# A new order for the first block's list of steps: attention units one by one, one gate later, recurrent preparation earlier

## The chip, the cores and the metric

The kernel runs on one core of one Trainium2 chip. The metric is device microseconds from start to end of the program. A core has five engines that run side by side, each through its own fixed sequence of instructions: TensorE (PE, matrix products), VectorE (DVE), ScalarE (ACT), GpSimd (POOL) and SyncE (SP, which issues the loads of the weights). They wait for each other through semaphores.

## What is computed

Two transformer-like blocks on one sequence of 256 tokens and width 1024, all in fp32. Only the first half of the first block is touched by the change:

```python
xn = rms_norm(x, norm1_w)
q, k_c, v_c, k_s, v_s, k_w, v_w, g_nsa, xr, gr, g_a, g_b = split(xn @ w_in)
attn = nsa_attention(q, ...)      # compressed + two causal branches, 8 heads
rnn = rg_lru_branch(xr, gr, ...)  # conv, gates, linear scan, times gelu(gr)
merged = sigmoid(g_a) * (attn @ w_up_attn) + sigmoid(g_b) * (rnn @ w_up_rnn)
x = x + merged @ w_out
```

The recurrent branch is `a = exp(c * r)`, `b = sqrt(1 - a^2) * (i * xc)`, `h[t] = a[t] h[t-1] + b[t]`, where `r` and `i` are sigmoids of small block products of the convolved input `xc` and `c` is a function of `lru_lambda` alone. The compressed attention needs a small two-layer network over the keys and values first. Behind this half come an MLP and the whole second block, which the change leaves alone.

## The kernel before

All products are made with operands split in two fp32r parts, a high and a low one, and three products each. The activations u are split once. The weights come in raw pieces of up to 128x1024, and each piece is split when it is wanted: ACT copies it to `whi` (line 260), DVE subtracts to get `wlo` (line 261). Five pieces of either can stand ready. PE then takes a product of 128 output rows pair by pair (`mmx`, line 324): a step such as `ga0` is 48 matmuls with 256 columns, and DVE (and for a gate ACT, a tanh) empties the PSUM bank.

The order of the first block is written by hand in `ORDER_1` (line 158), a string of words. Each word becomes a step (or several), and the steps are called one after the other; their weight blocks are packed into pieces in the same order. The list does not fix the order of the instructions: the program is built under `tile.TileContext(nc, schedule_with_timeline_sim=True)`, which orders the instructions of each engine at build time, by what it expects to be ready, with the order of the calls as priority. Where the kernel wants an order for certain it ties one instruction behind another of the same engine (`behind`, no semaphore).

The words:

- `xr0` to `xr3`, `gr0` to `gr3`, `ga0` to `ga3`, `gb0` to `gb3`: products with w_in, two column blocks each. `ga` and `gb` are the gates of the attention and of the recurrent branch, `xr` and `gr` the input and the gate of the recurrent one.
- `cmp_x`, `cw0` to `cw7`, `cmp_hT`, `cmp_fin`, `cmp_w2`, `cmp_attn`: the compression network and its attention (scores `cmps`, one exponential, probabilities).
- `atN`: the next N units of a queue of sixteen attention units. With j from 0 to 3 (pairs of heads) a unit is s0j or s1j (`nsa_scores`: scores of the first or second half of the tokens in the PSUM banks "s", of which there are two; a minimum per row on DVE, line 824; exponentials on ACT through line 287, six for s0j and two for s1j; scaling on DVE, line 835) or t0j or t1j (`nsa_T`: transposes on PE, line 843, then the split `pt..h` on ACT, line 354, and `pt..l` on DVE, line 355). The queue is s00 s10 t00 s01 t10 s11 t01 s02 t11 s12 t02 s03 t12 s13 t03 t13. Unit t0j reads s0j alone, unit t1j reads s0j and s1j.
- `pv`: the next of four products of probabilities and values (line 909); the second and the fourth also add the compressed part and split the result into `q`.
- `prep` (`rnn_prep`, line 921): c from lru_lambda, 27 small steps on POOL with 8 columns each, two sigmoids on ACT and three small steps on DVE; its first step is tied behind the norm's power on POOL.
- `lru0` to `lru3`: block products into the banks "s", two sigmoids each (ra, ig), a tanh with c (rt). Then `exp` (ra again, squares, rt), `sqrt` (rt), `bt` (xc, line 1003), `gelu` (rg), and `scan0` to `scan3`: two scans (line 1015), a product with rg (line 1016), and the split into `rnn` (lines 354 and 355).
- `mb0` to `mb3` (m1b, reads all of rnn) and `ma0` to `ma3` (m1a, reads q): the upward projections.

ACT has one table of functions loaded at a time. `G.table` (line 287) therefore puts the calls into groups by table, in the order of the list, and ties each call behind every call of the group before. Tanh is in several tables and joins the group that is open; copies and squares are free.

Of the kernel before, what the change touches and what calls it, by code (L numbers as in the profile page):

```python
# [10 lines left out]
AF = mybir.ActivationFunctionType  # L11
# [3 lines left out]
P = 128  # L15
# [139 lines left out]

ORDER_1 = """norm cst xr0 kv_fin q_fin k0 ties q1 cmp_x ga0 cw0 vg0 cw1 xr1 cw2 at1 ga1 cw3 prep cw4 xr2 cw5 at1 ga2 cw6 cw7 xr3 cmp_hT cmp_fin
cmp_w2 gr0 cmp_attn at2 lru0 lru1 ga3 at1 lru2 lru3 at1 gr1 at1 gr2 pv0 at1 gr3 exp sqrt bt at1 gelu gb0 pv0 at1 scan0 at1
scan1 gb1 gb2 scan2 at2 scan3 gb3 at1 mb0 at1 mb1 pv0 at1 mb2 pv0 mb3 ma0 ma1 ma2 ma3"""  # L160
ORDER_2 = """qs0 qs1 qe0 qe1 nb ka0 ka1 va at1 qb0 at1 qb1 at2 kb at3 ga0 at3 ga1 at3 ga2 at3 ga3 at3 gb0 at2 gb1 at2 gb2 at1
ma0 gb3 ma1 mb0 ma2 mb1 ma3 mb2 mb3"""

# [31 lines left out]
class Prog:  # L195
# [154 lines left out]
    def split2(self, hi, lo, src, scale=1.0):  # L350

        nc = self.nc
        if isinstance(scale, float) and scale == 1.0:
            nc.scalar.activation(out=hi, in_=src, func=AF.Copy)
            nc.vector.tensor_tensor(out=lo, in0=src, in1=hi.bitcast(F32), op=ALU.subtract)
        else:
            nc.scalar.activation(out=hi, in_=src, func=AF.Copy, scale=scale)
            nc.vector.scalar_tensor_tensor(out=lo, in0=src, scalar=scale, in1=hi.bitcast(F32), op0=ALU.mult, op1=ALU.subtract)


    def fm(self, tag, name, nk, npair, x, evac, rows=None, cols=None, lead=2, hold=2, after=None):
# [38 lines left out]
def build(nc, tc, d, out, es, dbg=None):  # L400
# [22 lines left out]
    G = Prog(nc, tc, pools, d, dbg)  # L423
    one = pools["one"]
    V = {}
    S = {}
# [410 lines left out]
    def probs_T(name, tiles, dst):  # L837

        for s in range(2):
            pt = G.ps("t", f"pt{name}{s}")  # L840
            ts = tiles(s)
            for e, t in enumerate(ts):
                nc.tensor.transpose(pt[:, e * P:(e + 1) * P], t, S["ident"])
            h, l = dst(s)
            G.split2(h, l, pt[:, :len(ts) * P])

    def rr_pair(name, n):
        return [[pools["rr"].tile([P, 768], F32R, tag="rr", name=f"{name}{s}{a}")[:, :n] for a in "hl"] for s in range(2)]
# [38 lines left out]
    def nsa_T(br, j):  # L887
        a = S[f"at0{j}"]
        if br == 0:
            tiles = lambda s: [a[:, s, 0:P], a[:, s, T:T + P], a[:, s, T + P:2 * T]]  # L890
        else:
            w = S[f"at1{j}"]
            tiles = lambda s: [a[:, s, P:T], w[:, s, 0:P], w[:, s, P:T]]
        if j % 2 == 0:
            S["pt", br] = rr_pair(f"pt{br}{j}", 768)
        c = 384 * (j % 2)
        probs_T(f"n{br}{j}", tiles, lambda s: [x[:, c:c + 384] for x in S["pt", br][s]])
# [107 lines left out]
    def rnn_gelu():  # L1005
        for h in range(2):
            sl = slice(4 * h, 4 * h + 4)
            G.table("gelu", out=S["rg"][:, sl, :], in_=S["rg"][:, sl, :], func=AF.Gelu_apprx_tanh)

    def rnn_scan(p):  # L1010
        sl = slice(2 * p, 2 * p + 2)
# [57 lines left out]
    def first():  # L1069

        rows = (("kcvc", lambda n: [((512, 640)[n], P)]), ("q", lambda n: [(n * 64, 64), (256 + n * 64, 64)]))

        def fn():
            S["kcvc"], S["q0"] = G.ps("g", "kcvc0"), G.ps("s", "q0")
            for k in range(8):
                ws = [(S[key][:, nn * T:(nn + 1) * T], *G.wt((tag, k, nn)), nn) for key, tag in (("kcvc", "kcvc"), ("q0", "q"))
                      for nn in range(2)]
                x = xu(k)
                for o, wh, wl, nn in ws:
                    for a in range(2):  # L1080
                        nc.tensor.matmul(o, wh, x[:, a, :], start=k + nn + a == 0, stop=False, skip_group_check=True)
                for o, wh, wl, nn in ws:
                    nc.tensor.matmul(o, wl, x[:, 0, :], start=False, stop=k == 7, skip_group_check=True)

        G.step(fn, [((tag, k, n), W1, [(k * P, P)], cols(n)) for k in range(8) for tag, cols in rows for n in range(2)])
# [49 lines left out]
    first()  # L1135
    for w in ORDER_1.split():
        if w in STEPS_1:
# [311 lines left out]
    def b2_T(kind, j):  # L1449
        nm_ = f"{kind}{j}"  # L1450
        t = S["at" + nm_]
        pts = S["pt" + nm_] = rr_pair("pt" + nm_, 512)
        probs_T(nm_, lambda s: [t[:, s, i * T + kb * P:i * T + (kb + 1) * P] for kb in range(2) for i in range(2)], lambda s: pts[s])
# [189 lines left out]
```

## Time and profile before

| | us |
|---|---|
| median of 3 runs | 967.04 (966.53 to 969.43) |
| the profiled execution | 966.44 |
| its span, first to last instruction | 964.7 |
| PE busy | 946.2 (98%) |
| DVE busy | 730.2 (76%) |
| ACT busy | 588.0 (61%) |
| mean granted PE clock | 0.994 |

A busy share is a mean over the whole span: the stage that the change touches lies in the first 230 us and is loaded otherwise than the rest. The granted clock is 1.00 at 2.4 GHz and 0.50 at 1.2 GHz. Consecutive matmuls overlap in the records, so that a matmul of 0.28 us may start 0.12 us behind the one before.

### The profile page before, as it was taken

The page shows a single profiled execution, that of the slowest core. Times are in us where ns is not written, and L with a number is a line of the kernel's source. Part 1 is how long each engine was busy: PE and PEld are TensorE (multiplying, and loading weights), DVE is VectorE, ACT ScalarE, POOL GpSimd, SP SyncE. Part 2 cuts the span into 40 slices and gives each one's busy share as a digit, 9 for nine tenths or more (in the row PEclk, how much of TensorE's full clock was granted, in tenths as well). Part 3 has the DMA queues.
Part 4 walks back from the last instruction along what each step waited for, and adds up shares of the span by engine and source line. Part 5 has one row for each costly group of instructions (what it writes and reads, how often), then busy time and mean ns, then how long its engine had stood idle before and what let it go on. Part 6 is the DMA issues. An engine that isn't in the chain of part 4 may idle for free.

```text
span 964.7 us, 15748 instructions
## 1 busy us (share of the span) xinstructions
PE 946.2 (98%) x6176; PEld 862.7 (89%) x6176; DVE 730.2 (76%) x1219; ACT 588.0 (61%) x966; POOL 46.6 (5%) x72
## 2 busy tenths in 40 slices
PE   9999997999999999999999999999999999999996
PEld 8999997998888888888888888999999888888885
DVE  7999779878787755569888666779877878878553
ACT  6896599446666644446555444588974566555541
POOL 1117000000000000021000200000000000000000
PEclk9999998999999999999999999999999999999999
DMA  9667342445545555557455755363334565555541
GB/s 337 227 222 259 131 176 88 158 137 188 199 176 184 203 181 175 190 185 227 175 197 196 212 197 190 125 232 124 126 132 135 175 226 186 193 199 173 180 158 43
DMA packets 28138, 174.01 MB, mean 180 GB/s; under 512 B 3488, under 2 KB 4768, under 8 KB 9120
## 3 DMA queue, kind: packets, MB, share of 16 engines
q1 hardware_dynamic: 26208, 169.07, 50.2%
q0 software_dynamic: 1136, 2.63, 1.3%
q10 hardware_dynamic: 720, 1.31, 0.4%
q8 instruction: 48, 0.79, 0.3%
q14 instruction: 26, 0.21, 0.1%
HBM read 171.43 MB, written 1.05 MB: 179 GB/s over the span
## 4 chain that ended last, share of the span: by engine, by line
PE 92%; ACT 4%; DVE 2%; issue 1%; DMA 0%; SPq 0%; POOLq 0%; POOL 0%; ACTq 0%
PE f L331 17%; PE w L331 12%; PE f L332 9%; PE w L332 6%; PE ld L318 6%; PE ga L324 5%; PE fd L331 4%; PE wo L331 3%; PE gb L324 3%; PE gr L324 2%; PE m1b L324 2%; PE fd L332 2%; PE xr L324 2%; PE wo L332 2%; PE va L318 1%; PE qa L324 1%
## 5 line engine op out<-in xcount | busy, mean ns | idle before, releaser
L261 DVE TENSOR_TENSOR wlo<-raw,whi 128x1024 fp32r<-128x1024 f32 (+2 forms) x326 | 388.6, 1196 | 167.7 <-ACT whi L260 148.6
L260 ACT ACTIVATE whi<-raw 128x1024 fp32r<-128x1024 f32 (+2 forms) x326 | 336.5, 1037 | 292.3 <-PE w L331 69.1
L331 PE MATMUL f<-u,whi 128*128 128x512 f32 x704 | 244.5, 393 | 0.0
L332 PE MATMUL f<-u,wlo 128*128 128x256 f32 x704 | 196.2, 279 | 0.0
L331 PEld LDWEIGHTS f<-u,whi 128*128 128x128 f32 x704 | 131.7, 187 | 29.5
L332 PEld LDWEIGHTS f<-u,wlo 128*128 128x128 f32 x704 | 132.7, 188 | 0.2
L331 PE MATMUL w<-hid,whi 128*128 128x512 f32 x256 | 90.5, 399 | 0.0
L331 PE MATMUL w<-u,whi 128*128 128x512 f32 x256 | 90.3, 398 | 0.0
L332 PE MATMUL w<-hid,wlo 128*128 128x256 f32 x256 | 71.9, 281 | 0.0
L332 PE MATMUL w<-u,wlo 128*128 128x256 f32 x256 | 71.7, 281 | 0.0
L331 PE MATMUL fd<-f1h,whi 128*128 128x512 f32 x176 | 61.1, 394 | 0.0
L331 PEld LDWEIGHTS w<-hid,whi 128*128 128x128 f32 x256 | 48.1, 188 | 12.0
L331 PEld LDWEIGHTS w<-u,whi 128*128 128x128 f32 x256 | 48.0, 188 | 11.6
L318 PE MATMUL ld<-whi,f2h 128*128 128x512 f32 x176 | 54.4, 390 | 0.0
L324 PE MATMUL gb<-u,whi 128*128 128x256 f32 x256 | 49.7, 286 | 0.0
L332 PE MATMUL fd<-f1h,wlo 128*128 128x256 f32 x176 | 48.8, 277 | 0.0
L332 PEld LDWEIGHTS w<-u,wlo 128*128 128x128 f32 x256 | 48.3, 189 | 0.1
L332 PEld LDWEIGHTS w<-hid,wlo 128*128 128x128 f32 x256 | 48.4, 189 | 0.0
L324 PE MATMUL ga<-u,whi 128*128 128x256 f32 x256 | 47.7, 283 | 0.0
L331 PE MATMUL wo<-m,whi 128*128 128x512 f32 x128 | 44.5, 396 | 0.0
L324 PEld LDWEIGHTS gb<-u,whi 128*128 128x128 f32 x256 | 40.6, 191 | 0.1
L324 PEld LDWEIGHTS ga<-u,whi 128*128 128x128 f32 x256 | 40.1, 191 | 0.0
(545 smaller groups left out, 1902.1 us busy)
## 6 DMA issues: line engine op xcount, KB each, us to landing
raw<-in_ws_dram SPq DMA_DIRECT2D x148, 1024.0 KB, 4.8
raw<-in_ws_dram SPq DMA_DIRECT2D x3, 960.0 KB, 4.8
raw<-in_ws_dram SPq DMA_DIRECT2D x9, 256.0 KB, 4.8
raw<-in_ws_dram SPq DMA_DIRECT2D x2, 992.0 KB, 4.8
nar<-in_rpb_dram POOLq DMA_DIRECT2D x16, 96.0 KB, 5.3
res<-in_x_dram SPq DMA_DIRECT2D x8, 128.0 KB, 4.2
raw<-in_ws_dram SPq DMA_DIRECT2D x2, 512.0 KB, 5.6
raw<-in_ws_dram SPq DMA_DIRECT2D x1, 932.0 KB, 13.0
```

What stands on the lines that cost most here:

```text
L260: self.hi_ins.append(nc.scalar.activation(out=hi[:, :w], in_=src, func=AF.Copy))
L261: self.lo_ins.append(nc.vector.tensor_tensor(out=lo[:, :w], in0=src, in1=hi[:, :w].bitcast(F32), op=ALU.subtract))
L318: mm(out, a, b, start=start and r == 0, stop=stop and r == 2, skip_group_check=True)
L324: ins = mm(out, a, b, start=start and r == 0, stop=stop and r == 2, skip_group_check=True)
L331: mm(bank.rearrange("p (a t) -> p a t", a=2), wh, x, start=start, stop=False, skip_group_check=True)
L332: mm(bank[:, :T], wl, x[:, 0, :], start=False, stop=stop, skip_group_check=True)
```

## The change

It rewrites `ORDER_1` and adds one tie. In the list: `prep` moves from behind `cw3` to ahead of `ga0`; the units t00, s01, t10 and s11 move up, t00 to behind `cmp_hT`, s01 ahead of `cmp_attn`, t10 behind it, s11 behind `gr1` and so ahead of `lru0`; `gr1`, `gr2` and `gr3` move up between the `lru` steps; `ga3` moves from behind `lru1` to behind `gr3` and the first `pv`; t11 stands ahead of `exp` instead of behind `bt`; the second `pv` stands ahead of `gb0`; the units s03 to t13 are listed one at a time between the products `gb1` to `mb1`. The tie: the two GELUs come behind ACT's last split of a transposed probability that was traced before them, which is that of t11.

```diff
-ORDER_1 = """norm cst xr0 kv_fin q_fin k0 ties q1 cmp_x ga0 cw0 vg0 cw1 xr1 cw2 at1 ga1 cw3 prep cw4 xr2 cw5 at1 ga2 cw6 cw7 xr3 cmp_hT cmp_fin
-cmp_w2 gr0 cmp_attn at2 lru0 lru1 ga3 at1 lru2 lru3 at1 gr1 at1 gr2 pv0 at1 gr3 exp sqrt bt at1 gelu gb0 pv0 at1 scan0 at1
-scan1 gb1 gb2 scan2 at2 scan3 gb3 at1 mb0 at1 mb1 pv0 at1 mb2 pv0 mb3 ma0 ma1 ma2 ma3"""
+ORDER_1 = """norm cst xr0 kv_fin q_fin k0 ties q1 cmp_x prep ga0 cw0 vg0 cw1 xr1 cw2 at1 ga1 cw3 cw4 xr2 cw5 at1 ga2 cw6 cw7 xr3 cmp_hT
+at1 cmp_fin cmp_w2 gr0 at1 cmp_attn at1 gr1 at1 lru0 lru1 gr2 at1 lru2 lru3 gr3 pv0 at1 ga3 at1 exp sqrt bt gelu pv0 gb0 at1 scan0 at1
+scan1 gb1 at1 scan2 at1 gb2 scan3 at1 gb3 at1 mb0 at1 mb1 pv0 mb2 pv0 mb3 ma0 ma1 ma2 ma3"""
...
 def split2(self, hi, lo, src, scale=1.0):
-            nc.scalar.activation(out=hi, in_=src, func=AF.Copy)
+            ins = nc.scalar.activation(out=hi, in_=src, func=AF.Copy)
...
+        return ins
...
 def probs_T(name, tiles, dst):
-            G.split2(h, l, pt[:, :len(ts) * P])
+            S["pt_ins"] = G.split2(h, l, pt[:, :len(ts) * P])
...
 def rnn_gelu():
-            G.table("gelu", out=S["rg"][:, sl, :], in_=S["rg"][:, sl, :], func=AF.Gelu_apprx_tanh)
+            G.behind(G.table("gelu", out=S["rg"][:, sl, :], in_=S["rg"][:, sl, :], func=AF.Gelu_apprx_tanh), S["pt_ins"])
```

## Rows read from the trace of the kernel before

**Rows 1.** The page, busy us of the span by engine

```profile
PE 946.2 (98%) x6176; PEld 862.7 (89%) x6176; DVE 730.2 (76%) x1219; ACT 588.0 (61%) x966; POOL 46.6 (5%) x72
```

**Rows 2.** Windows: stretch, length, busy us by engine (instructions), PE clock, DMA share, GB/s

```profile
48.00:64.00 16.00, 14.20 (x118) 13.79 (x117) 15.15 (x38) 15.40 (x31) 2.15 (x3) 1.00 0.62 216
64.00:84.00 20.00, 20.00 (x171) 20.00 (x171) 18.72 (x37) 16.34 (x23) 7.60 (x14) 1.00 0.74 253
84.00:116.00 32.00, 32.00 (x269) 31.83 (x268) 26.61 (x55) 15.65 (x30) 11.82 (x14) 1.00 0.55 195
116.00:158.00 42.00, 41.89 (x347) 41.39 (x345) 34.38 (x88) 41.33 (x80) 0.00 (x0) 1.00 0.36 126
158.00:172.00 14.00, 6.72 (x29) 5.55 (x30) 14.00 (x37) 13.40 (x35) 0.00 (x0) 0.76 0.28 90
172.00:200.00 28.00, 28.00 (x227) 27.43 (x226) 19.50 (x41) 11.04 (x15) 0.35 (x2) 1.00 0.46 166
```

**Rows 3.** Waits of PE over the whole run: for whom, us, times, longest

```profile
PE o L909 <- ACT pt100h L354: 3.6, 1, 3.6
...
PE cmph L713 <- ACT whi L260: 1.8, 1, 1.8
```

**Rows 4.** Timeline of PE: start, us, instruction, idle before it and its releaser

```profile
157.61 0.28 PE L324 MATMUL gb<-u,wlo 128*128 128x256 f32 x1
...
165.55 0.79 PE L324 MATMUL m1b<-rnn,whi 128*128 128x256 f32 x2 [2.12 <-ACT rnn L354]
...
171.50 0.39 PE L324 MATMUL m1b<-rnn,whi 128*128 128x256 f32 x1 [1.69 <-DVE rnn L355]
```

**Rows 5.** Windows of 2 us, columns as in rows 2

```profile
166.00:168.00 2.00, 2.00 (x9) 1.60 (x8) 2.00 (x4) 2.00 (x8) 0.00 (x0) 0.50 0.86 340
```

**Rows 6.** Timeline of ACT, 140 to 165 (exponential of s11, splits, squares, GELU)

```profile
140.72 0.50 ACT L287 ACTIVATE attn<-attn,nmn 128x256 f32<-128x256 f32 x1
...
141.21 0.47 ACT L354 ACTIVATE pt001h<-ptn 128x384 fp32r<-128x384 f32 x1
141.58 0.62 ACT L992 ACTIVATE asq<-ra 128x512 f32<-128x512 f32 x1
...
154.66 2.01 ACT L287 ACTIVATE rg<-rg 128x1024 f32<-128x1024 f32 x2
...
160.95 0.47 ACT L354 ACTIVATE pt100h<-ptn 128x384 fp32r<-128x384 f32 x1
...
164.88 0.62 ACT L354 ACTIVATE rnn<-rg 128x512 fp32r<-128x512 f32 x1
```

**Rows 7.** Timeline of ACT, 114 to 118 (last exponentials of s01, the sigmoids' table)

```profile
114.51 0.40 ACT L287 ACTIVATE attn<-attn,nmn 128x128 f32<-128x128 f32 x1 [0.41 <-DVE nmn L824]
...
115.90 1.28 ACT L287 ACT_TABLE_LOAD   x1
```

**Rows 8.** Timeline of DVE, 151 to 172

```profile
151.48 1.29 DVE L1003 TENSOR_TENSOR xc<-xc,rt 128x512 f32<-128x512 f32 x2 [1.28 <-ACT rt L287]
...
159.76 0.68 DVE L1016 TENSOR_TENSOR rg<-xc,rg 128x512 f32<-128x512 f32 x1
...
165.05 0.53 DVE L355 TENSOR_TENSOR pt100l<-ptn,pt100h 128x384 fp32r<-128x384 f32 x1
165.50 0.68 DVE L1015 TENSOR_TENSOR_SCAN xc<-ra,xc 128x256 f32<-128x256 f32 x1
...
170.76 1.28 DVE L355 TENSOR_TENSOR rnn<-rg,rnn 128x512 fp32r<-128x512 f32 x2
```

**Rows 9.** Steps of the preparation's tile sp_w: ns min/median/max, first and last start

```profile
L940 POOL TENSOR_SCALAR sp_w<-sp_w x9: 231/339/4330, 80.3 to 94.8; 128x8 f32<-128x8 f32 x9
...
L935 DVE RECIPROCAL sp_z<-sp_w x1: 194/194/194, 76.9 to 76.9; 128x8 f32<-128x8 f32 x1
```

**Rows 10.** Windows of line 261 alone (wlo splits): stretch, length, DVE busy us (instructions)

```profile
76.00:97.00 21.00, 11.78 (x10) 1.00 0.71 240
97.00:118.00 21.00, 6.11 (x5) 1.00 0.42 151
```

More of the change, by code (lines that the diff above doesn't have):

```diff
@@ L353, in split2 @@
         if isinstance(scale, float) and scale == 1.0:
-            nc.scalar.activation(out=hi, in_=src, func=AF.Copy)
+            ins = nc.scalar.activation(out=hi, in_=src, func=AF.Copy)
             nc.vector.tensor_tensor(out=lo, in0=src, in1=hi.bitcast(F32), op=ALU.subtract)
         else:
-            nc.scalar.activation(out=hi, in_=src, func=AF.Copy, scale=scale)
+            ins = nc.scalar.activation(out=hi, in_=src, func=AF.Copy, scale=scale)
             nc.vector.scalar_tensor_tensor(out=lo, in0=src, scalar=scale, in1=hi.bitcast(F32), op0=ALU.mult, op1=ALU.subtract)
+        return ins
     def fm(self, tag, name, nk, npair, x, evac, rows=None, cols=None, lead=2, hold=2, after=None):
```

## The prediction

> **What bounds the kernel now.** I read five views in this order. The page first: TensorE (PE) is busy 98% of the span [rows 1], so only its few holes can be won; everything else it does must be done anyhow. The windows by stretch show where they are: PE loses about 1.8 us in 48 to 64 and 7.3 us in 158 to 172, where its clock also averages 0.76, and next to nothing between 64 and 158 [rows 2]. The waits of PE name the holes: one on a high part of weights (whi) for the compression, 1.8 us, and one on the probabilities pt100h, 3.6 us [rows 3]; the timeline of PE adds the rest, 2.12 us for the high part of rnn and 1.69 us for its low part [rows 4]. The last gate product ends at 157.89 and the recurrent projection m1b runs freely only from 171.50 [rows 4]. In these 13.6 us PE ran 29 instructions instead of the rate of 116 to 158, 347 in 42 us, or 0.121 us each [rows 2]: 29 x 0.121 = 3.5 us of work, so about **10 us are lost**, 7.4 us of them as waits and the rest to the half clock (0.50) [rows 5].
>
> What PE lacks at 158 is not work in an earlier place but rnn, which ACT and DVE have late. Their load is the reading that matters: in 84 to 116 ACT is busy 15.65 of 32 us and DVE 26.61; in 116 to 158 ACT is busy 41.33 of 42; in 158 to 172 DVE 14.00 of 14; after 172 both have room again [rows 2]. The recurrent chain runs through just this full part: sigmoids, exponentials, roots, scans, GELU, splits. **The bound of the stage is ACT up to the roots and DVE behind them.** PE's products run out at the same time whatever their order, since before m1b the list holds the same twelve gate products and recurrent inputs in both kernels.
>
> **The change, part by part.** The list is a priority: the framework orders every engine's instructions when the program is built, so a word that moves may move its instructions less or not at all.
>
> *Attention units ahead of the recurrent gates.* Unit t00 moves before the compression's end, s01 before its attention, t10 and s11 before lru0. What leaves ACT's full stretch: the four splits of t00 and t10 at 0.37 us each and the two exponentials of s11 at 0.49 us each, counted from start to start [rows 6], together 4 x 0.37 + 2 x 0.49 = 2.46 us. The table group of the gates' sigmoids also opens a little earlier: what ends just ahead of its load is now s11 with 2 x 0.49 = 0.98 us where the second half of s01 took 115.90 - 114.51 = 1.39 us [rows 7]; 0.4 us. So the roots, and the products bt that wait for them at 151.48 [rows 8], come **2.85 us earlier**. On DVE the same units leave 116 to 150, where it has 7.6 us idle in 42 [rows 2]; nothing is gained there, since bt waited for ACT.
>
> Where they go there is room on ACT (16.35 us idle in 84 to 116). DVE has 32 - 26.61 = 5.4 us idle there [rows 2], and it needs four low splits at about 0.45 us [rows 8] for t00 and t10, 1.8 us, and something like 2 us for s11, an estimate from its two exponentials' width and that split. It just fits, and I count it at nothing; if it does not fit, the compression slips (the rival that ends slower).
>
> *t11 ahead of the exponentials, GELU tied behind its split.* Today GELU starts at 154.66 and pt100h is split at 160.95 [rows 6]; the tie turns them round. The two low splits of t11, 165.05 to 165.50 and one more like it, sit on DVE ahead of the first low split of rnn at 170.76 [rows 8]; they leave, **0.9 us**. The wait of 3.6 us [rows 3] goes, but what is late next is rnn itself, so this alone brings no more. The tie adds a wait: behind GELU on ACT queue the next gate's tanh, the last table load, s12's exponentials and rnn's high splits. It costs nothing while t11's transposes are ready, and s11 scaled by about 120 (an estimate, behind its new exponentials) covers that by some 30 us; without that cover it costs up to 161.3 - 154.7, nearly 7 us.
>
> *ga3 late, gr1 to gr3 early.* The same PE work, DVE product and tanh in another place; its tanh stays ahead of the roots. Nothing: PE has a product to run at every point before 158 [rows 2]. The weight blocks are repacked in the new order, in as many loads; nothing.
>
> *Preparation before ga0.* No DMA goes with it. Its two small sigmoids and its reciprocals of 0.19 us [rows 9] come into 40 to 64, where ACT is busy 15.40 of 16 and PE waits for it [rows 2, 3]; four such steps at 0.19 less what overlaps, I take 0.2 us of loss, bounds 0 and 0.8. It no longer parts two groups of exponentials, so two table loads of 1.28 us [rows 7] go from 64 to 84; PE waits for nothing there (20.00 of 20) [rows 2], so that is worth nothing. The values are wanted by the gates' tanh only, long after, so early values gain nothing. On POOL its 27 steps now stand ahead of the copies of the attention gates, which the scaling of s00 needs; that is used by t00 more than 20 us later, which hides some 5 us.
>
> *Those steps beside DVE.* Now they fall into a stretch where DVE has 0.85 us idle in 16 [rows 2]. In today's place the wlo splits take 11.78/10 = 1.18 us beside them and 6.11/5 = 1.22 us after them [rows 10], while a POOL step of 0.23 us stretches to 4.33 us [rows 9]: POOL gives way. So I charge nothing. The Trainium skill, "SBUF — State Buffer" (SBUF: two separate sides), says that the two share a port pair as an exclusive lock and that whichever starts first blocks the other fully. By it DVE would lose too, which is the last rival; the stretched POOL steps agree with the page, the unhurt DVE splits do not show its other half.
>
> *The clock.* A wait that stays may find PE cold. Before, the half clock was over when m1b ran freely. If the new wait is one piece, 2 us at 0.50 [rows 5] cost 1 us of work; ends 0 and 1.0, and I take 0.4, nearer to 0 because units still drop into the gap as they do now.
>
> **Sum.** Against the profiled execution's own 966.44 us (its span of 964.7 and 1.7 around it; 0.6 under the median of 967.04): -2.85 - 0.90 + 0.20 + 0.40 = -3.15, **963.3 us**. About 6 of the 10 us stay as a wait for rnn.
>
> **Rivals.** *The gap closes.* The product that feeds rnn's first split is made at 159.76, the high split follows only at 164.88 and the low one at 170.76 [rows 8, 6]: some 9 us of mere queueing behind attention and weight splits. If the new order puts these splits next to their product, all 10 us go, and the early 1.8 us may too: 954.5 to 959, say 957. For it: nothing of the data forbids it. Against: s03 is now listed ahead of scan2, and with it more DVE work.
>
> *The order hardly differs, or DVE takes back what ACT gives.* DVE is busy without a break from 151.5 to 172, and if the new emission puts s03 or s13 ahead of rnn, 2 to 3 us come back: 964.2 to 968. Today's trace supports it: s11 is listed right behind lru3, yet its exponentials run among those of the recurrent part, at 140.72 [rows 6].
>
> *Slower: the sigmoids start late.* lru now shares its table group and its two PSUM banks with what is listed ahead, s11 and the compressed scores. The load stands at 115.90 [rows 7]; every us of delay moves the full ACT behind it by as much. If the 5.4 us of idle DVE do not take the moved units, compression, s11 and lru slip together; from about 4 us on the change loses, at 7 to 8 us it gives 970 to 971.
>
> *POOL holds up DVE.* If 27 steps held it for 0.23 us each [rows 9], 6.2 us less its 0.85 idle, some 5 us, would go to PE's hole at 57: about 968.
>
> **How the numbers follow.** Forecast 0.42 (961.5 to 965, a quarter of it above 964.1), closed gap 0.24, order hardly different 0.17, late sigmoids 0.13, POOL 0.04. A measurement of this kernel can tell some 0.3%, 2.9 us, from no change: faster is below 964.1. Faster 0.32 + 0.24 = 0.56; same 0.10 + 0.17 + 0.04 = 0.31; slower 0.13. The range 956.5 to 968.0 leaves out the late sigmoids and a piece of the closed gap, under 2 in 10.
>
> **What would show it.** Right: s11's exponentials before the first sigmoid load, that load at 115 to 116, bt near 148.6, pt100h split before GELU, the 3.6 us wait gone, and one wait for rnn ending near 167.7. Wrong: a load past 119; rnn's splits right behind their product; a PE wait at 57 longer than 2.2 us; or new waits of PE between 84 and 158.

## The result and the profile after

The change makes the kernel **slower**: 977.63 us (977.22 to 979.92, 4 runs) against 968.18 us before on the same chip (966.53 to 969.43, 4 runs), a ratio of 1.0103 with a 95% interval of 1.0079 to 1.0128. The forecast was 963.3 us in a range up to 968.0, so sign and range are both wrong. The profiled execution of after took 979.92 us, its span 978.1 us; 1.9 us of its distance to the profile of before lie ahead of the change, since its first gate product starts at 31.53 us instead of 29.67. The ratios here and below leave out two disturbed executions (1887 us in run 5, 1897 us in run 2) and are not exactly the quotients of the medians.

The page of after, busy us by engine, answers to [rows 1]:

```profile
PE 951.1 (97%) x6176; PEld 868.1 (89%) x6176; DVE 731.3 (75%) x1219; ACT 586.5 (60%) x964; POOL 40.5 (4%) x72
```

The work is the same; ACT has two instructions fewer, the table loads that the early preparation no longer needs. Of the 13.4 us by which the span grew, 8.5 are idle time of PE (978.1 - 951.1 = 27.0 us, before 964.7 - 946.2 = 18.5), and 4.9 are PE's busy time for the same 6176 instructions, which ran more often at the lower clock. The windows of after, in the stretches and columns of [rows 2], say where:

```profile
48.00:64.00 16.00, 10.75 (x64) 10.34 (x64) 10.57 (x29) 13.83 (x29) 0.00 (x0) 0.79 0.35 103
64.00:84.00 20.00, 20.00 (x171) 20.00 (x170) 18.97 (x52) 17.15 (x40) 1.98 (x4) 1.00 0.58 205
84.00:116.00 32.00, 32.00 (x268) 31.83 (x268) 29.61 (x52) 17.28 (x23) 0.00 (x0) 1.00 0.72 258
116.00:158.00 42.00, 42.00 (x349) 41.60 (x348) 29.47 (x69) 31.63 (x66) 0.00 (x0) 1.00 0.36 126
158.00:172.00 14.00, 11.19 (x92) 10.86 (x90) 13.97 (x38) 13.25 (x23) 0.00 (x0) 1.00 0.36 121
172.00:200.00 28.00, 18.56 (x125) 17.56 (x126) 24.31 (x55) 19.26 (x42) 0.00 (x0) 0.76 0.32 113
```

Two stretches lost. In 48 to 64 PE ran 64 instructions where it ran 118, and its clock fell to 0.79. And the late hole has moved from 158 to 172 into 172 to 200. The row between them is the telling one: in 116 to 158 ACT, which was full (41.33 of 42), now idles for 10 us. The waits of PE in after, answering to [rows 3]:

```profile
PE Sn L866 <- ACT k L623: 5.2, 2, 2.7
PE ptn L844 <- DVE pt021l L355: 4.5, 1, 4.5
PE ptn L844 <- DVE pt020l L355: 4.3, 1, 4.3
PE m1b L324 <- ACT rnn L354: 3.0, 1, 3.0
...
PE m1b L324 <- DVE rnn L355: 0.5, 1, 0.5
```

The wait for pt100h is gone, as was said, and that for the compression's weights is gone too. In their place stand 5.2 us for the halves of the keys, and 12.3 us in four pieces ahead of m1b (before: 3.6 + 2.1 + 1.7 = 7.4). The timeline of PE in after, answering to [rows 4]:

```profile
168.91 0.28 PE L324 MATMUL gb<-u,wlo 128*128 128x256 f32 x1
...
173.46 0.33 PE L844 MATMUL ptn<-ident,attn 128*128 128x128 f32 x1 [4.26 <-DVE pt020l L355]
...
178.25 0.44 PE L844 MATMUL ptn<-ident,attn 128*128 128x128 f32 x1 [4.47 <-DVE pt021l L355]
...
181.71 1.01 PE L324 MATMUL m1b<-rnn,whi 128*128 128x256 f32 x3 [3.01 <-ACT rnn L354]
...
183.22 0.58 PE L324 MATMUL m1b<-rnn,whi 128*128 128x256 f32 x1 [0.51 <-DVE rnn L355]
```

**The early loss** stands on POOL's queue. Its timeline in after (the steps of the preparation, then the copies of keys and values into the compression's buffer cmpA, then what follows):

```profile
24.38 0.72 POOL L926 TENSOR_SCALAR rp<-vec 128x8 f32<-128x8 f32 x1
...
42.93 0.48 POOL L945 TENSOR_TENSOR rp<-sp_w,rp 128x8 f32<-128x8 f32 x1
43.36 0.78 POOL L603 DMA_DIRECT2D cmpA<-kv_sb  x1
...
45.26 0.59 POOL L604 DMA_DIRECT2D cmpA<-kv_sb  x1
```

In before the same queue held nothing ahead of the first of these issues but the wait for its data:

```profile
26.12 0.76 POOL L602 DMA_DIRECT2D cmpA<-kv_sb  x1 [2.36 <-DVE kv_sb L596]
```

Four DMA issues start 17 us later, though `kv_fin`, the word that issues them, stands ahead of `prep` in both lists. DVE's step that makes kv_sb ends at 27.7 us in after, so for nearly 16 us the issues wait for nothing that the trace shows but the POOL steps in front of them. Why the program was built in this order is not recorded; the likely reason is that at build time kv_sb was not expected to be ready yet and the preparation was. ACT pays next (timeline of after):

```profile
49.99 1.28 ACT L354 ACTIVATE cmpB<-cmpA 128x120 fp32r<-128x120 f32 x4 [5.50 <-DMA cmpA<-kv_sb]
```

Behind these waiting steps queue the key halves that the first scores need; the first of them starts at 51.3 us.

**The late loss** is a recurrent chain that starts late. On DVE's timeline of after stand the compression's first step and the products bt:

```profile
100.12 0.28 DVE L732 COPY cmp_hid<-cmphT 128x128 f32<-128x128 f32 x1
...
165.85 1.29 DVE L1004 TENSOR_TENSOR xc<-xc,rt 128x512 f32<-128x512 f32 x2
```

On ACT's, the compression's tanh, the last exponential of s11 and the sigmoids' table:

```profile
113.21 0.29 ACT L744 ACTIVATE cmp_u<-cmp_u 128x128 f32<-128x128 f32 x1
...
129.90 0.51 ACT L287 ACTIVATE attn<-attn,nmn 128x256 f32<-128x256 f32 x1 [1.32 <-DVE nmn L825]
...
130.52 1.28 ACT L287 ACT_TABLE_LOAD   x1
```

The same first step and tanh in before, on the same two timelines:

```profile
88.58 0.27 DVE L731 COPY cmp_hid<-cmphT 128x128 f32<-128x128 f32 x1
```

```profile
97.77 0.29 ACT L743 ACTIVATE cmp_u<-cmp_u 128x128 f32<-128x128 f32 x1
```

The compression starts 11.5 us late and takes 3.9 us more to its tanh; s11's second exponential, right ahead of the sigmoids' load, waits for DVE; the load stands at 130.5 instead of 115.9 [rows 7] and bt at 165.9 instead of 151.5 [rows 8]. The delay of 14.6 us, 1.9 of them from the late start, arrives there almost whole (14.4).

### The profile page after: what moved, and what is told of

The parts are those of the page before. It is cut to its first block, busy times and chain, and to the rows that moved or that the text cites. A ratio compares the mean times of both kernels' runs of the same rounds, so it can differ in the third digit from the quotient of the medians.

```text
span 978.1 us, 15746 instructions
## 1 busy us (share of the span) xinstructions
PE 951.1 (97%) x6176; PEld 868.1 (89%) x6176; DVE 731.3 (75%) x1219; ACT 586.5 (60%) x964; POOL 40.5 (4%) x72
## 4 chain that ended last, share of the span: by engine, by line
PE 92%; DVE 3%; ACT 2%; POOL 1%; DMA 1%; issue 1%; POOLq 0%; SPq 0%; ACTq 0%
PE f L331 17%; PE w L331 12%; PE f L332 8%; PE w L332 6%; PE ld L318 6%; PE fd L331 4%; PE ga L324 4%; PE gb L324 3%; PE wo L331 3%; PE m1b L324 3%; PE xr L324 2%; PE gr L324 2%; PE fd L332 2%; PE wo L332 2%; PE va L318 1%; PE qa L324 1%
## 5 line engine op out<-in xcount | busy, mean ns | idle before, releaser
L331 PEld LDWEIGHTS f<-u,whi 128*128 128x128 f32 x704 | 131.7, 187 | 29.6
L331 PEld LDWEIGHTS w<-u,whi 128*128 128x128 f32 x256 | 48.0, 188 | 11.6
```

What stands on the lines that cost most here:

```text
L331: mm(bank.rearrange("p (a t) -> p a t", a=2), wh, x, start=start, stop=False, skip_group_check=True)
```

## The experiments

Twelve kernels ran. In the lists of words, parts that stay are left out. One table for all: start of the first product ga0 (where a profile begins late or early), of the compressed scores, of the first sigmoids' table load and of GELU, the last product of m1b, all in us of the profiled run, then the median of all runs and the ratio to before.

| kernel | ga0 | scores | sigmoids | GELU | last m1b | us | ratio, 95% |
|---|---|---|---|---|---|---|---|
| before | 29.7 | 108.4 | 115.9 | 154.7 | 201.0 | 966.5 to 968.2 | 1 |
| after | 31.5 | 124.0 | 130.5 | 170.8 | 214.4 | 977.6 | 1.0079 to 1.0128 |
| 1 preparation early | 30.5 | 113.1 | 122.2 | 164.3 | 211.1 | 976.4 | 1.0085 to 1.0119 |
| 2 change, prep. tied | 30.4 | 116.2 | 123.5 | 163.0 | 205.6 | 971.1 | 1.0030 to 1.0063 |
| 3 change, prep. back | 30.7 | 119.0 | 127.4 | 166.4 | 208.1 | 972.8 | 1.0050 to 1.0080 |
| 4 roots first | 29.6 | 108.3 | 115.8 | 152.1 | 203.2 | 969.0 | 1.0011 to 1.0033 |
| 5 prep. early, tied | 30.5 | 107.6 | 115.2 | 154.1 | 199.9 | 965.2 | 0.9968 to 0.9988 |
| 6 units, compression | 30.2 | 119.0 | 123.6 | 162.2 | 204.2 | 969.5 | 1.0016 to 1.0035 |
| 7 units, gates | 30.4 | 109.1 | 121.0 | 158.8 | 205.8 | 970.5 | 1.0016 to 1.0039 |
| 8 tail | 29.6 | 109.8 | 117.3 | 158.5 | 206.5 | 970.9 | 1.0025 to 1.0055 |
| 9 ga3 late | 29.6 | 108.2 | 115.8 | 157.0 | 203.1 | 969.5 | 1.0014 to 1.0035 |
| 10 t11 early | 29.6 | 109.8 | 117.4 | 156.1 | 202.5 | 967.0 | 0.9989 to 1.0008 |
| 11 s03 behind rnn | 30.0 | 108.6 | 116.1 | 155.0 | 200.1 | 963.9 | 0.9956 to 0.9981 |
| 12 rnn first | 29.7 | 106.8 | 114.3 | 156.9 | 197.6 | 964.1 | 0.9954 to 0.9977 |

The profiled executions of runs 8, 10 and 11 stand some 1.5 us late from 64 us on, and not by their lists: from ga0 to the scores runs 8 and 10 take 80.2 us where before takes 78.7, and run 11 takes 78.6 where run 5 takes 77.1. All five have the wait of 1.8 us for the compression's weights, which ends at 59 to 60. Behind it PE's clock stays at 2.4 GHz in before and in run 5; in the three it falls to 1.2 GHz after another 1.5 us or so of products, for some 3.3 us. The stretch of [rows 2] in run 10, then in run 11:

```profile
48.00:64.00 16.00, 14.20 (x106) 13.80 (x105) 15.16 (x38) 14.81 (x31) 2.19 (x3) 0.90 0.62 215
48.00:64.00 16.00, 14.21 (x108) 13.80 (x107) 14.83 (x38) 15.79 (x36) 9.75 (x24) 0.91 0.60 209
```

Their later times are therefore compared below from the scores or the load on.

**1. The early preparation alone, on before.**

```diff
-... cmp_x ga0 ... cw3 prep cw4 ...
+... cmp_x prep ga0 ... cw3 cw4 ...
```

> The kernel before with one edit: prep moved ahead of ga0, nothing else. Theory A (the whole loss comes from POOL's queue: the preparation's steps now stand ahead of the four copies of the compression's keys and values, which POOL has to issue, so cmp_x, the second half of k and q and with them PE wait): those copies are issued at 41 to 45 us instead of 26, PE loses some 7 us between 44 and 62, and the time is 974 to 979, ratio to the kernel before 1.008 to 1.012. Theory B (the moved attention units make the sigmoids late, the preparation costs little): 966 to 969. Theory C (both share): 970 to 973.

As theory A expected, the copies are issued at 42.3 to 44.2 us, and the time falls into its range. This one word of the list loses as much as the whole change. The waits of PE show both halves of the loss, the keys early and rnn late:

```profile
PE m1b L324 <- ACT rnn L354: 8.2, 1, 8.2
PE Sn L865 <- ACT k L622: 5.4, 2, 2.9
```

The units were not moved here, and yet the sigmoids' load is 6.3 us late: in the hole DVE is busy for 6.2 of the 12 us from 44 to 56 (before 11.6), and the compression, whose steps run there, comes late with the rest of its work (scores at 113.1).

**2. The whole change, with the preparation's third POOL step tied behind the four copies.**

```diff
-        nc.gpsimd.tensor_tensor(out=tb, in0=tb, in1=tc_, op=ALU.mult)
+        G.behind(nc.gpsimd.tensor_tensor(out=tb, in0=tb, in1=tc_, op=ALU.mult), S["kv_ins"])
```

> The changed kernel with one tie more: the third POOL step of the preparation, the first behind its sigmoids, comes behind POOL's last copy of keys and values. The preparation stays early, ahead of ga0, and it stays beside DVE in the full stretch. Theory A (POOL's queue): copies at 26 to 29 us again, no new wait of PE at 44 to 60, 965 to 970. Theory D (not the queue, but POOL's steps hold up DVE or ACT in the full stretch, wherever they stand): still 973 or more. Theory B (the units): 975 or more, with the sigmoids' table load as late against the products as now.

The copies are issued from 26.8 us, no wait for the keys is left, and 6.5 us come back, against theory D. About 4.6 us of loss stay, 1 us more than theory A allowed: PE waits 11.3 us ahead of m1b (before 7.4), 8.4 of them in one piece for pt021l. They are the list's, not the queue's. The two pieces make 11.1 us, more than the 9.5 of the result, since the median of before was 968.2 there and is 966.5 here.

**3. The whole change, with the preparation in its old place.**

```diff
-... cmp_x prep ga0 ... cw3 cw4 ...
+... cmp_x ga0 ... cw3 prep cw4 ...
```

> The changed kernel with prep put back behind cw3; units, late gate and the tie of GELU stay. Theory A: 965 to 969 and, if the units and the late gate are worth the 3 us that were forecast, 962 to 965; the hole of PE ahead of m1b is read from the trace: 10 us lost as in the kernel before if they are worth nothing. Theory B: 974 or more.

Some 5 us come back by this other way, 1.7 less than with the tie. The two intervals overlap, but run 5 and before differ by as much, in the same direction. The time fits neither range of the expectation: POOL's queue was about half of the loss, not all of it.

**4. Roots, GELU and scans one after the other, the late units behind them.**

```diff
-... pv0 at1 gr3 exp sqrt bt at1 gelu gb0 pv0 at1 scan0 at1 scan1 gb1 gb2 scan2 at2 scan3 gb3 at1 mb0 at1 ...
+... pv0 gr3 exp sqrt bt gelu scan0 scan1 scan2 scan3 gb0 at2 pv0 gb1 at1 gb2 at1 gb3 at1 mb0 at3 ...
```

> The kernel before with another list behind pv0: exp sqrt bt gelu scan0 to scan3 are listed ahead of the units s02 and t11 and of gb0, and the other units behind them one by one up to mb1. If the hole ahead of m1b is queueing of the recurrent chain behind attention work on ACT and DVE (the reading of the profile before, and the rival in which the gap closes), m1b starts within 4 us of the end of the last gate product and the time falls to 957 to 962. If the hole only moves to the attention's end, ahead of m1a, 964 to 970. If ACT and DVE are simply full whatever the order: 966 to 969.

rnn's first split starts at 156.0 instead of 164.9 [rows 6], 9 us sooner, 0.24 us behind the product that feeds it, and the kernel is some 2 us slower. PE waits no less, only for others, since probabilities and gates now come late:

```profile
PE o L909 <- ACT pt100h L354: 3.4, 1, 3.4
PE gb L324 <- DVE tgb L1024: 2.1, 1, 2.1
PE o L909 <- DVE pt100l L355: 2.0, 1, 2.0
```

So rnn's queueing alone is not what was lost before the change: PE needs all of it, the attention of the second pair too.

**5. Before, with the early preparation and the tie of run 2.**

```diff
-... cmp_x ga0 ... cw3 prep cw4 ...
+... cmp_x prep ga0 ... cw3 cw4 ...
...
-        nc.gpsimd.tensor_tensor(out=tb, in0=tb, in1=tc_, op=ALU.mult)
+        G.behind(nc.gpsimd.tensor_tensor(out=tb, in0=tb, in1=tc_, op=ALU.mult), S["kv_ins"])
```

> The kernel before, with the preparation alone ahead of the first gate product, its third POOL step bound behind the issue of the four copies of keys and values. Theory of the POOL queue: all that the early preparation lost came through those four issues, so with them in front again the copies start at 26 to 28 us, PE does not wait for the scores' k, the sigmoids' table loads near 116, and the time is 966 to 968.5 us. Rival, the small sigmoids and reciprocals on ACT and DVE cost by themselves what comes after (late compression): the load stands at 119 or later and the time is 970 to 974.

The whole loss of run 1 hangs on these four issues: with them in front the early preparation is a gain of 1.2 to 3.1 us, better than the theory's 966 to 968.5. Its POOL timeline:

```profile
26.95 0.77 POOL L602 DMA_DIRECT2D cmpA<-kv_sb  x1 [2.35 <-DVE kv_sb L596]
...
29.45 1.24 POOL L930 TENSOR_TENSOR rp<-rp 128x8 f32<-128x8 f32 x1
```

The rest of the preparation runs from 46 to 59, beside DVE. Its group of weight splits there (ns, least, median and most):

```profile
L261 DVE TENSOR_TENSOR wlo<-raw,whi x5: 1212/1224/1226, 49.8 to 56.4; 128x1024 fp32r<-128x1024 f32 x5
```

In before, without POOL beside them, six of them in 49 to 59 have a median of 1220 ns. POOL gives way (its steps of 0.20 to 0.25 us stretch to 1.0 to 1.24 here and there) and DVE does not; the wait of 1.8 us for the compression's weights is the same in both.

**6 and 7. The units alone, on before:** t00 and s01 into the compression, then t10 and s11 ahead of the gates.

```diff
-... cmp_hT cmp_fin cmp_w2 gr0 cmp_attn at2 lru0 ...
+... cmp_hT at1 cmp_fin cmp_w2 gr0 at1 cmp_attn lru0 ...
```

> The kernel before, with only t00 moved ahead of the compression's end and s01 ahead of its attention; the preparation, t10, s11 and ga3 as before. Theory of the slipping compression: DVE has no room for the two units beside the compression's steps, so the compressed scores come at 112 to 117 instead of 108.4, the sigmoids' load at 119 to 124, the time is 968.5 to 971. Rival, what costs is the gate left for the end and the units one by one behind it: the load stays within 1.5 us of 115.9 and the time within 1.5 us of before.

```diff
-... cmp_attn at2 lru0 lru1 ga3 at1 lru2 lru3 at1 gr1 ...
+... cmp_attn at2 at1 at1 lru0 lru1 ga3 lru2 lru3 gr1 ...
```

> The kernel before, with only t10 and s11 moved ahead of the recurrent gates (lru0); all else as before. Theory of the slipping compression: these two units stand behind it, so the compressed scores stay at 108 to 109, the sigmoids' load moves by less than 2 us, s11's exponentials leave the full stretch of ACT, and the time is 964.5 to 967.5. Rival, s11 ahead of lru holds the sigmoids by the table group and the PSUM banks that they share: load at 119 to 122, time 968.5 to 971.

Run 6 is the compression's slip: its steps on DVE stand between the low splits of t00 and those of weights, and the compressed scores come 10.6 us late, at 119.0, later than the 112 to 117 that were expected; load and time fall into the theory's ranges.

```profile
94.20 0.28 DVE L731 COPY cmp_hid<-cmphT 128x128 f32<-128x128 f32 x1
94.40 0.54 DVE L355 TENSOR_TENSOR pt000l<-ptn,pt000h 128x384 fp32r<-128x384 f32 x1
...
98.09 0.35 DVE L735 TENSOR_TENSOR cmp_hid<-cmp_hid 128x60 f32<-128x60 f32 x2
...
100.09 0.55 DVE L355 TENSOR_TENSOR pt001l<-ptn,pt001h 128x384 fp32r<-128x384 f32 x1
```

Run 7 leaves them at 109.1 and still loads the sigmoids 5.1 us late, 0.7 of them from a later start. There the rival of its expectation holds, not the slip: lru, which needs the banks "s", starts at 118.8 instead of 114.3, behind s11's products in the same banks, and ahead of the load ACT has 0.86 us of idle time, a weight split, an exponential of the moved units and ga3's tanh (timeline):

```profile
118.92 1.06 ACT L260 ACTIVATE whi<-raw 128x1024 fp32r<-128x1024 f32 x1 [0.86 <-ACT attn L287]
119.88 0.49 ACT L287 ACTIVATE attn<-attn,nmn 128x256 f32<-128x256 f32 x1
...
120.37 0.62 ACT L287 ACTIVATE tga<-tga 128x512 f32<-128x512 f32 x1
121.01 1.28 ACT L287 ACT_TABLE_LOAD   x1
```

**8, 9 and 10. The tail alone, on before:** all of it, then ga3 alone, then t11 alone.

```diff
-... lru0 lru1 ga3 at1 lru2 lru3 at1 gr1 at1 gr2 pv0 at1 gr3 exp sqrt bt at1 gelu gb0 pv0 at1 ...
+... lru0 lru1 at1 lru2 lru3 at1 gr1 at1 gr2 gr3 pv0 at1 ga3 at1 exp sqrt bt gelu pv0 gb0 at1 ...
```

> The kernel before, with only the tail of the change's list: the gate product ga3 as the last one ahead of the exponentials, t11 ahead of them, the units behind them one by one; the preparation and the four units ahead of the gates as before, no tie. Theory of the slipping compression: the loss lies ahead of this, so the load stays at 115 to 117 and the time is 963.5 to 967.5. Rival, the tail itself loses (ga3's tanh, product and splits in the full stretch of ACT, the wait for pt021l at the end): load unchanged, roots and GELU 3 us later or more, time 969 to 972.

```diff
-... lru1 ga3 at1 ... gr3 exp ...
+... lru1 at1 ... gr3 ga3 exp ...
```

> The kernel before, with the gate product ga3 alone moved: last ahead of the exponentials instead of between lru1 and lru2. If the tail's loss of 4 us is ga3's (its product on DVE, its tanh and its splits of weights now inside the full stretch of ACT and DVE), this run gives most of it: GELU 2 us later or more, 968.5 to 971. If it is t11 ahead of GELU, this run stays at 966 to 968 with GELU within 1 us of 154.7.

```diff
-... gr3 exp sqrt bt at1 gelu ...
+... gr3 at1 exp sqrt bt gelu ...
```

> The kernel before, with the unit t11 alone moved from between bt and GELU to ahead of the exponentials. If t11 ahead of GELU is the tail's loss (its two splits on ACT ahead of GELU, 2 x 0.37 us, and its low splits ahead of bt on DVE), GELU comes 0.7 us or more later and the time is 968 to 970. If ga3 is the loss, this run keeps what the forecast hoped for: the wait for pt100h gone and 964.5 to 967.

Some 4 us are lost by the tail and over half of that by ga3 alone, with the sigmoids' load of run 9 where it was; that of run 8 is late by the clock's fall alone. t11 alone changes nothing: GELU follows the sigmoids' load by 38.8 us as in before, its place in the list did not put its split ahead of GELU, and the wait of 3.6 us stayed. In run 9 that split did come ahead of GELU; its timeline of ACT between the two roots and GELU:

```profile
150.26 1.06 ACT L287 ACTIVATE rt<-rt 128x1024 f32<-128x1024 f32 x1
151.23 0.61 ACT L992 ACTIVATE asq<-ra 128x512 f32<-128x512 f32 x1
151.75 1.04 ACT L260 ACTIVATE whi<-raw 128x1024 fp32r<-128x1024 f32 x1
152.70 0.47 ACT L354 ACTIVATE pt100h<-ptn 128x384 fp32r<-128x384 f32 x1
153.07 0.47 ACT L354 ACTIVATE pt101h<-ptn 128x384 fp32r<-128x384 f32 x1
153.44 1.06 ACT L260 ACTIVATE whi<-raw 128x1024 fp32r<-128x1024 f32 x1
154.60 1.06 ACT L287 ACTIVATE rt<-rt 128x1024 f32<-128x1024 f32 x1
```

The first root starts when it did (150.39 before), but a square, two splits of t11 and a second split of weights stand before the second one, where before has one split of weights: GELU is 2.3 us late, and PE's waits for rnn are 7.2 and 1.8 us, 9.0 against 7.4 with the wait for pt100h. What that wait gave back was paid with interest.

**11. Run 5, and the scores of s03 held behind rnn's low split** (its masked minima on DVE, by a tie; they are listed behind that split but were emitted ahead of it).

```diff
+            if name == "n03":
+                G.behind(ins, S["rnn_ins", 1][1])
```

> The kernel with the early preparation tied behind the copies (965.2 us), and the scores of unit s03 held behind the low split of rnn's second pair on DVE. Theory of the queue: rnn's splits come 3 to 5 us after their product only because s03's six masked minima on DVE (2.3 us) and its exponentials on ACT (2 us) stand ahead of them; with them behind, the low split comes 1.5 to 2.5 us sooner, the waits of m1b for rnn shrink by as much, and the time is 962.5 to 964.5. Rival, s03 is itself what the next hole waits for (t03, the second output): the waits move behind m1b and the time is 965 to 967.

**12. Run 11, and besides GELU tied behind t11's splits, half of the bt products made with their scans, and these scans behind rnn's low split.**

```diff
-        for p in range(4):
+        for p in range(2):
             nc.vector.tensor_tensor(out=pair(S["xc"], p), in0=pair(S["xc"], p), in1=pair(S["rt"], p), op=ALU.mult)
...
+        if p > 1:
+            nc.vector.tensor_tensor(out=pair(S["xc"], p), in0=pair(S["xc"], p), in1=pair(S["rt"], p), op=ALU.mult)
...
+            if p > 1:
+                G.behind(ins, S["rnn_ins", 1][1])
```

> The same as the kernel with s03 behind, and besides: GELU tied behind the splits of t11, the products bt of the second half made with their scans, and these scans behind rnn's low split of the second pair. Theory of the queue: PE no longer waits for pt100h (2.2 us) and rnn's low splits come another 2 to 3 us sooner; 960 to 963. Rival: the late half of the scans and of rnn now comes too late for m1b's second half, a new wait m1b for rnn of 1 us or more behind the first, and the time is 963.5 to 967.

Both are faster than before and after; the two can't be told apart. Run 11 falls into its theory's range. Counted from the scores, rnn's low split comes 1.9 us sooner than in run 5 (168.75 - 108.57 against 169.74 - 107.62), and PE's wait of 1.2 us for it is gone, though that for the high split is 2.6 us instead of 2.2. The intervals of runs 5 and 11 overlap, so the 1.3 us between their medians are not shown to be a gain. Run 12 falls into the range of its rival, though not by the rival's mechanism: its wait of 1.0 us behind the first is for a low split of the first half, at 165.66. Waits of PE in run 12:

```profile
PE o L912 <- DVE pt100l L355: 1.4, 1, 1.4
PE m1b L324 <- DVE rnn L355: 1.0, 1, 1.0
```

The 2.2 us for pt100h turn into 1.4 for pt100l, and rnn's high split is no sooner (164.13, in run 5 164.27), because GELU behind the tie starts at 156.9.

## Why the prediction was wrong

**"Preparation before ga0. No DMA goes with it."** True of the step, false of the queue that it was moved past: the prediction looked for what queues behind the preparation on POOL and named the copies of the attention gates alone, not the four issues of `kv_fin`. The list has these first, and the prediction took that for the order of the queue, though it says itself that the list is only a priority. This is the step that failed first: it was sized at 0.2 us of loss, with 0.8 as its bound, and costs 9.9 by itself (run 1), 6.5 within the change (run 2), as four issues that wait 17 us on POOL; tied, it gains (run 5). That it can gain was not foreseen either: with run 5's early preparation the table of the exponentials follows the sigmoids' load by 18.7 us instead of 19.9 (133.90 - 115.17; 135.84 - 115.90). Whether this comes from the two table loads that are gone, which were put at nothing, or from another order of the instructions was not taken apart.

**"2.85 us earlier", the units ahead.** This rested on a condition that was counted "at nothing": that 5.4 us of idle DVE between 84 and 116 take the moved units. DVE did the work; in after it still has 2.4 us idle there. But idle time in a window is not a free place at the right moment. The compression is a chain of short steps, each of which queues behind whatever stands next on DVE or ACT, mostly a weight split of 1.2 us, and each added split lengthens the chain (run 6). So bt came 14.4 us late instead of 2.85 early. And the exponentials of s11 did run ahead of the load, as said, but there the second waits 1.3 us for its minimum in after, right ahead of the load; for 0.98 us saved behind the load, run 7 has the load 5.1 us later.

**ga3 late, counted as "Nothing"**, failed: 2.7 us in the medians (run 9). PE did have a product at every point, as the step argued; ACT's order between the roots is what changed. **t11 ahead, "0.9 us"**: nothing alone (run 10). With ga3 late its split does come ahead of GELU, without the tie (runs 8 and 9), and both runs lose; what the tie does within the change was not tried by itself. **The clock**, 0.4 us, was about right for the late hole: m1b's start from 181.7 to 187.6 runs at 1.2 GHz, (5.9 - 0.5)/2 = 2.7 us of work, where 2.6 to 3.2 were lost to it before (10 or 10.6 less the waits of 7.4); its fall to a mean of 0.79 in 48 to 64 belongs to the hole that was not foreseen. Of the 29 instructions that the prediction sets against 13.6 us, 4 run behind 171.5 by PE's timeline: so the loss in that hole was nearer 10.6 us than 10, which changes no term of the sum.

Of the signs named as right, three came true (s11 ahead of the load, t11's split ahead of GELU, the 3.6 us gone) without the time. Of the signs named as wrong, the load past 119 came true (130.5), and PE's new waits, 2.7 and 2.5 us, came before 57, at 49 to 55.

**The rivals.** "Slower: the sigmoids start late" is what happened in the second loss, with its mechanism and its sign "a load past 119"; it had 0.13 and a price of 970 to 971 for a load 7 to 8 us late. Run 2 has the load 7.6 us late and takes 971.1 us, and the units alone give 969.5 and 970.5 (runs 6 and 7). No rival had the POOL queue. "POOL holds up DVE" is excluded by run 5's weight splits (1224 ns beside POOL, 1220 without). The Trainium skill, "SBUF — State Buffer" (SBUF: two separate sides), would have both engines block each other in turn; here only POOL's side of it is seen. "The gap closes" did not come from the one list that puts rnn's first split next to its product (run 4): there PE waits for probabilities and gates instead, so to bring one part forward put another back. Holding back work that PE does not want yet (run 11) took away one wait; its gain is not clear of noise.

**The parts don't add.** Runs 1, 6, 7 and 8 lose 9.9, 2.6, 3.6 and 4.1 us, 20 in all; the change, which has them all, loses 9.5 (11.1 against the 966.5 of run 2's comparison). They delay the same chain; that what is late for one reason waits no longer for the next is the likely reason, not a tested one. That chain is no full measure either: GELU is 7.5 us late in run 6 and the kernel 2.6, probably since the moved units are done by then and leave the hole's own work shorter.

Open: by which of its steps the whole list loses 4.6 us where its parts lose 10, and why copies issued late land late (below); neither was tried.

## What to carry to other kernels

When a step moves up in a list that a scheduler orders, look at each queue that it uses for DMA issues that are not ready yet: here ready work was put first, and the issues, with the whole chain behind the copies, waited for it. One tie put them back in front. Before units are moved into "idle" time, follow the longest chain of short steps through that window; here it paid for the instructions put between them, with idle time left in the window. And in a hole where PE wants several results, bringing one of them forward (run 4) gained nothing; postponing what is not wanted yet (run 11) is worth a trial.

## What was not expected of the hardware

The same four POOL copies of 128 KB take longer from issue to landing when they are issued late. The tile's row in after, and in before:

```profile
DMA to landing us min/median/max: 5.3/5.6/6.2
```

```profile
DMA to landing us min/median/max: 2.7/2.9/3.2
```

That is 2.7 us of the early loss besides the 17 of queueing. The Trainium skill, "SBUF — State Buffer" (SBUF: two separate sides), says that a DMA issued from POOL can be starved while DVE runs certain operations. The trace speaks against it as the cause here: DVE was busy for all of 26 to 31 in before, where the copies were fast, and for 4.29 of 8 us in 43 to 51 in after, where they were slow. Another reason was not tried: a load of weights that runs beside the copies. SP issues one at 42.78 in after, 0.6 us ahead of the first copy, and one at 41.73 in run 1, whose copies take 5.6 to 6.3 us; in before the next one is issued at 28.70, behind all four. Over the whole stretch the DMA engines were no busier (share 0.64 in 43 to 51, 0.76 in 26 to 31).
